# Letting the builder order a two-block network by its timeline simulation

## The chip, the cores and the metric

One core of a Trainium2 chip runs the whole network. The metric is the device time of one execution in microseconds, as the median of the runs shown; less is better.

## The reference

The input is 512 tokens of 1024 channels in float32. The first block has two layers; each mixes the tokens in four groups of 256 channels (RWKV7 "A", differential attention "B", spatial gating "C", forgetting attention "D") and goes through a gated feed-forward part with a short convolution. The second block has one layer: gated linear attention over the tokens and a context of 256, and a mixture of 16 experts, two to a token. Both blocks are modulated by six vectors each, made from a condition by a 1024 by 6144 product.

```python
# first block, for each of two layers
mod = cond @ ada_w[l] + ada_b[l]
h = _rms_norm(x, norm1_g[l]) * (1.0 + sc1) + sh1
pa, pb, pc, pd = _split(h @ w_in[l], GROUP_COLS)
y = jnp.concatenate([ya, yb, yc, yd], axis=-1)     # the four mixers
x = x + g1 * (y @ w_out[l])
h = _rms_norm(x, norm2_g[l]) * (1.0 + sc2) + sh2
x = x + g2 * _conv_glu_ffn(h, ffn_up[l], ffn_conv[l], ffn_conv_b[l], ffn_down[l])
# second block
y_lat = _gla_mixer(h, hc, w_in, w_ga, w_gb, b_g, norm_g, w_out, ctx_out)
x = x + g1 * y
for e in range(N_EXPERTS):
    he = jax.nn.silu(h @ w1[e]) * (h @ w3[e])
    out = out + gates[:, e:e + 1] * (he @ w2[e])
return _rmsnorm(x + g2 * out, final_g)
```

## The kernel before

The kernel is written as a program of tiles: it names the engine of each instruction and the tiles that it reads and writes. The builder then makes one queue of instructions for each engine. To find the order in a queue, the builder plays the program through in a simulation of its own: whenever an engine can take an instruction there, it takes, of those whose inputs are there and whose output has a free buffer, the one that stands first in the program. What the simulated clock says of the length of each instruction thus decides which of two independent instructions comes first. The order is fixed when the program is built, and each engine is handed its queue in that order. Buffers are given out in the order that the simulation finds as well.

The kernel leaves the order to the builder in some places and ties it in others.

- `weave` writes the steps of several generators into the program in turn, so many of one to so many of another (`W_A`, `W_B`, `W_P`, `W_D`, `START`). It makes the program order, and so the rank, of the parts of a mixing stage; it does not fix the queue.
- `first_write` links the first writers of all tiles of one tag: no buffer of a tag is taken ahead of its turn. Tags are linked each for itself; between two tags there is no link.
- In the stage of the experts, the loads of weights are linked one behind the other on SyncE's queue (`load`, `self.loaded`), a few instructions are linked behind a named one (`behind`, `self.normed`, `self.placed`), and the arithmetic of the routing and of the final norm stands in `tc.manual_schedule(engines={Act, DVE})`, where ScalarE and VectorE keep the order as written.

```python
# first_write, with tag the (pool, tag) of the tile that is written for the first time
if tag in self.chain:
    self.tc.add_manual_dep(ins, self.chain[tag], NOSYNC, reason="slots in program order")
self.chain[tag] = ins.name
# mix: the steps of mixer A beside the attention steps, the other projections and the modulations
weave((a_steps, W_A[l]), (then(b_mix, d_mix), W_D[l]), (then(d_project, lambda: a_pair(1), c_mix, close), W_P[l]),
      *([(self.filling(FILL[l]), FILL[l])] if FILL[l] else []), others=True)
weave((a_steps, W_B[l]), (most_out(), 8))
# kernel
with tile.TileContext(nc) as tc:
    network(tc, A, out[0])
```

The stages follow each other: modulation and norm (0 to 130 us), the mixers of layer 0 (130 to 529), its feed-forward part (541 to 927), the mixers of layer 1 (985 to 1366), its feed-forward part (1390 to 1779), gated linear attention (1806 to 2165), the routing (to 2238), the experts (to 2545) and the end.

All products with weights are made from two parts: a weight piece of 512 KB is loaded to `wraw` (or `e_w`), ScalarE casts it to `whi`, VectorE subtracts to get `wlo`, and TensorE makes three products for each pair of operands, into PSUM tiles of the tag `mm`. There are three buffers each of `wraw`, `whi`, `wlo` and `mm`.

In a mixing stage, mixer A is one long chain of small steps for each of two pairs of heads (`mixer_a`): products into tiles of the tag `sa`, each followed by VectorE or ScalarE on tiles `ka`, `a_W`, `a_st`, `X`, then the next small product; in the middle a detour over memory to GpSimd and back (`an_d`, `a_nb`, `t_d`). The scores of the attention mixers B and D go to tiles of the tag `sm`. The projections (`mm`) are the work that can be put between. Every instruction is issued through one wrapper, so the profile puts almost all of them on line 122; they are told apart by the names of their tiles.

Of the kernel before, what the change touches and what calls it, by code (L numbers as in the profile page):

```python
# [29 lines left out]
P = 128  # L30
# [18 lines left out]
# the share of each part of a layer's mixers in turn  # L49
# [60 lines left out]
class Engine:  # L110
    """an engine whose instructions take the tiles of a tag in program order"""
# [31 lines left out]
def weave(*parts, rounds=None, others=False):  # L143
    """steps of several parts in turn; parts: (generator, its number of steps), which yield True while they wait for another;
    rounds: stop when the last part has made that many; others: stop when the first part alone is left"""
    parts = [[g, n, 0] for g, n in parts]
    first, last = parts[0], parts[-1]
    while parts and not (others and parts == [first]):
        for x in sorted(parts, key=lambda q: q[2] / q[1]):
            x[2] += 1  # L150
            try:
                if next(x[0]):
                    x[2] -= 1
                    continue
            except StopIteration:
                parts.remove(x)
            break
        if rounds and last[2] > rounds:
            return


class Modulation:
    """columns r0..r1 of silu(c) @ w + b, 512 channels at a time; parts: (silu(c), last row, column tile) each"""
# [10 lines left out]
    def at_once(self, r0, r1):  # L174
        """eight columns of a single part: r0.. by TensorE, r1.. by VectorE"""
# [31 lines left out]
    def step(self, shared=False):  # L207
        """the sums over partitions of the last four columns, and the products of the next four (shared: by ScalarE and GpSimd, for a single part)"""
# [34 lines left out]
class Net:  # L243
# [46 lines left out]
    def unordered(self, x):  # L290
        """for a tile whose users wait for nothing that comes after it"""
        self.pending.pop(x.tensor.name if hasattr(x, "tensor") else x.name)

    def first_write(self, out, r):
        """the first writers of the tiles of a tag issue in program order, so that no slot is taken ahead of its turn"""
# [10 lines left out]
    def behind(self, **after):  # L306
        """what an engine does in here comes after the named instruction"""
# [20 lines left out]
    def scratch(self, tag, n=S):  # L328
        """2 KB in each partition"""
# [11 lines left out]
    def m4(self):  # L341
        """4 KB in each partition, for mixers B, C and D"""
        return self.t(self.mp, [P, 4 * GW], F32, "m4", self.bufs["m4"])

    def rsqrt(self, x, w, tag="rs"):
        """1/sqrt of a small [128, w] tile, by Newton steps from a bit-level seed"""
# [41 lines left out]
    def a_lora(self, mp, lo):  # L388
        """tanh of the decay inputs (rows 0-31), the a inputs (rows 32-63) and sigmoid of the gate inputs (rows 64-127)"""
# [8 lines left out]
    def mixer_a(self, pool, jj, r, k, v, th, prm, lora, lng, lnb, done):  # L398
        """in steps; done(y) takes the result [128 tokens, tile, 128 channels]"""
# [44 lines left out]
        # k' = k (1 + (a - 1) k_a), a = tanh / 2 + 1/2  # L444
# [169 lines left out]
    def diagonal(x):  # L614
        """the [16, 16] blocks on the diagonals of eight [128, 128] matrices in DRAM, 129 rows apart"""
# [3 lines left out]
    def a_blocks(self, pool):  # L619
        """(I - N)^-1 of the diagonal blocks of the eight strictly lower triangular N, and its transpose, by substitution on GpSimd"""  # L620
# [20 lines left out]
    def a_inverse(self, q, anT):  # L641
        """the transpose of (I - N)^-1 for four of the N (anT: transposed), by merging blocks"""
# [30 lines left out]
    def group_rms(self, x, groups, width, tag):  # L673
        """1/rms of each group of columns, [128, groups]"""
# [9 lines left out]
    def rope_tables(self, pool, qg, kg):  # L684
        """[128, tile, (q, k), 32] tables of cos * g and of the signed sin * g of the partner"""
# [16 lines left out]
    def b_qk(self, i, m, x, tabs, qkT):  # L702
        """x: q (i = 0) or k (1) of the token tiles 2m and 2m + 1 [128, 2 x 256]; their roped transposes go to qkT [128, 4, 512]"""
# [17 lines left out]
    def to_rows(self, x, out, scale=1.0):  # L721
        """two token tiles of 256 channels [128, 2 x 256] to [128, 2, 256] by channel"""
# [6 lines left out]
    def softmax(self, ps, N, mx, lsum, p):  # L729
        """p = exp(ps - max), with its row sums"""  # L730
# [4 lines left out]
    def weigh(self, po, z, p, nb, v):  # L735
        """values v by the weights p [128 queries, 128 nb keys], by channel, to half z of po [2 x 64, 128]"""
# [24 lines left out]
    def b_attend(self, i, qkT, v, nlam, oT):  # L761
        """one block of 128 queries; v: [128, tile, 256]; oT: [128, pair of heads, 512]"""
# [29 lines left out]
    def b_norm(self, oT, g):  # L792
        """rms norm of each head, in place; oT: [128 (two heads), pair, 512]"""
# [31 lines left out]
    def mixer_c(self, m, x, wT, lng, lnb, sgb, out):  # L825
        """x: v of the token tiles 2m and 2m + 1 [128, 2 x 256]; the mixed values by channel to out [128, 2, 512]"""
# [36 lines left out]
    def d_forget(self, ps, fb):  # L863
        """ps: forget logits [head, 512]; the summed log gates, negated, in three bf16 parts [3, head, 512] at partitions 0 and 64"""
# [43 lines left out]
    def w_split(self, ap):  # L908
        """ap: [rows, n] in DRAM; for each 128 rows the two parts [128, n]"""
# [17 lines left out]
    def mm3(self, ps, w, x, start, stop):  # L927
        """ps += w^T x for operands split in two parts"""
# [14 lines left out]
    def cond(self, aps):  # L943
        """silu of vectors of 1024 as columns [128, 8]"""
# [13 lines left out]
    def squares(self, x, kc):  # L958
        """adds up the squares of the channel tiles; with the last, their means by token [128, 8] (PSUM), in two parts"""
# [19 lines left out]
    def rms_tokens(self, pc, tag="nm"):  # L979
        """1/rms of each token [128, 4] from the means of squares"""  # L980
# [6 lines left out]
    def rms_rows(self, pc):  # L987
        """the same in every partition [128, 512] (PSUM)"""
# [7 lines left out]
    def norm_mod(self, x, pq, g, sc, sh, hi, lo):  # L996
        """hi + lo = rms_norm(x) g (1 + sc) + sh; pq: the sums of squares"""
# [22 lines left out]
    def project_rows(self, w, h, m, ntok=S, skip=None):  # L1020
        """one tile of 128 output channels: [128, ntok] = (w columns m)^T h, without the input tile skip"""
# [8 lines left out]
    def project_tokens(self, w, h, n, ps, c0, cols):  # L1030
        """one tile of 128 tokens by `cols` output channels"""
# [43 lines left out]
    def bcast(self, pool, tag, ap, n):  # L1075
        """a vector of n in every partition"""
# [4 lines left out]
    def mix(self, l, h, prm, mp, X, new_y, mods):  # L1081
# [14 lines left out]
        # columns: r 0-255, k 256-511, v 512-767, (wd, ad, gd) 768-895  # L1096
# [5 lines left out]
        def by_token(c0, use):  # L1102
            """256 columns for the pairs of token tiles"""
# [16 lines left out]
        def a_done(j):  # L1120
            """y[j]: [128 tokens, tile, 128 channels] to channel tile j of yT"""
# [29 lines left out]
        sgb = self.t(mp, [P, 2, P], F32, "sgb")         # the bias of the two heads of a pair, in their partitions  # L1151
# [81 lines left out]
        def most_out():  # L1233
            """x + g1 (y w_out) without the channels of the second pair of heads of A"""
# [65 lines left out]
    def fill(self, n, shared=False):  # L1300
        """goes on with the modulations that later parts need"""
# [50 lines left out]
    def load_x(self, src, X, ntok):  # L1352
        """tokens by channel [ntok, 1024] to X [128, 8, ntok]"""
# [11 lines left out]
    def gla_low(self, h, wga, ntok, tag):  # L1365
        """low-rank gate inputs, direction z in rows 32z..32z+15"""
# [8 lines left out]
    def gla_gate(self, low, wgb, bg, hd, z, ntok, out, chunk):  # L1375
        """prefix sums in chunks of 16 times the log decay min(x, 0) - ln(1 + exp(-|x|)); out [128, chunks, chunk + 1], with a leading 0"""
# [18 lines left out]
    def gla_context(self, T, mods, g, put):  # L1395
        """the context normed and modulated, by channel, in steps; put takes its two parts"""
# [36 lines left out]
    def gla_state(self, k, v, pre, S0):  # L1433
        """the states of one head after the context in both directions, in steps; k by channel, v by token"""
# [21 lines left out]
    def gla(self, X, pq, mods, mods_c, cols, new_x):  # L1456
        """X + g1 * mixer(X); X by channel"""
# [3 lines left out]
        with tc.tile_pool(name="gla", bufs=1, reuse_waits="tile") as gp:  # L1461
            T = lambda shape, tag, bufs=1, dt=F32: self.t(gp, shape, dt, "g_" + tag, bufs)
            self.mp, self.bufs = gp, dict(kb=8)
            # memory in the order in which the weights of the experts can have it
# [20 lines left out]
            # one table set with exp and ln, in place of a switch for each  # L1485
# [12 lines left out]
            def silu(ps, out):  # L1498
                """x / (1 + exp(-x)) with the functions of that set; below -80 it is 0"""
# [10 lines left out]
            def feed(hd):  # L1510
                """what head hd needs, in steps"""
# [52 lines left out]
            def result(hd):  # L1564
                """the output of a head by channel, in two parts"""
# [9 lines left out]
            def most_out():  # L1575
                """x + g1 (y w_out) without the channels of the last head"""
# [25 lines left out]
            # what the mixture of experts adds to: a row for each token, and more for the empty slots  # L1602
# [18 lines left out]
    def gla_head(self, gp, hd, q, k, pre, S0, vt, rt):  # L1621
        """one head: its normed and gated output replaces its columns of rt"""
# [7 lines left out]
        # between tiles: decayed keys by token, decayed queries by channel  # L1630
# [27 lines left out]
        # scores [key, tile, query]: every pair of tokens of a tile at the level where their halves part  # L1658
# [34 lines left out]
        # the diagonal, once from each direction  # L1693
# [44 lines left out]
    NE = 16  # L1738
    XB = 7      # the most blocks of 128 tokens that the experts can need beyond one each
# [717 lines left out]
```

## Time and profile before

| | |
|---|---|
| runs | 2612.86 and 2592.25 us, median 2602.56 |
| span of the profiled execution, first to last instruction | 2605.9 us |
| TensorE busy | 2331.5 us (89%) |
| TensorE's weight loads busy | 1865.2 us (72%) |
| VectorE, ScalarE, GpSimd busy | 1724.7, 1072.7, 415.7 us |
| mean granted TensorE clock | 0.913 |

A time of its own for the profiled execution is not given; its span lies between the two runs, 3.3 us above their median. Busy shares are of the span. "PE" is TensorE's matmuls, "PEld" its weight loads, "DVE" VectorE, "ACT" ScalarE, "POOL" GpSimd, "SP" SyncE, whose queue issues nearly all loads; a granted clock of 1.00 is 2.4 GHz and 0.50 is 1.2 GHz.

### The profile page before, as it was taken

The page shows a single profiled execution, that of the slowest core. Times are in us where ns is not written, and L with a number is a line of the kernel's source. Part 1 is how long each engine was busy: PE and PEld are TensorE (multiplying, and loading weights), DVE is VectorE, ACT ScalarE, POOL GpSimd, SP SyncE. Part 2 cuts the span into 40 slices and gives each one's busy share as a digit, 9 for nine tenths or more (in the row PEclk, how much of TensorE's full clock was granted, in tenths as well). Part 3 has the DMA queues.
Part 4 walks back from the last instruction along what each step waited for, and adds up shares of the span by engine and source line. Part 5 has one row for each costly group of instructions (what it writes and reads, how often), then busy time and mean ns, then how long its engine had stood idle before and what let it go on. Part 6 is the DMA issues. An engine that isn't in the chain of part 4 may idle for free.

```text
span 2605.9 us, 33466 instructions
## 1 busy us (share of the span) xinstructions
PE 2331.5 (89%) x12050; PEld 1865.2 (72%) x12050; DVE 1724.7 (66%) x3404; ACT 1072.7 (41%) x1704; POOL 415.7 (16%) x388
## 2 busy tenths in 40 slices
PE   6979889989999988989998999998988885888896
PEld 3767566778888776756676778886887763666685
DVE  5545575577647575455456873765667787898987
ACT  2424445244334342332424432434544433656664
POOL 1212232000000001000100000000222123555712
PEclk7878789989999987887898999998999998999998
DMA  7522234236545542110222563643311035899994
GB/s 243 151 72 74 74 102 133 81 97 183 154 121 182 163 126 60 26 31 27 72 73 67 157 191 110 184 140 110 98 34 48 25 130 202 290 309 321 320 321 104
DMA packets 336872, 352.23 MB, mean 135 GB/s; under 512 B 34006, under 2 KB 245658, under 8 KB 336570
## 3 DMA queue, kind: packets, MB, share of 16 engines
q1 hardware_dynamic: 330922, 330.59, 39.8%
q0 software_dynamic: 5776, 19.42, 3.3%
q8 instruction: 97, 1.59, 0.3%
q14 instruction: 77, 0.63, 0.1%
HBM read 324.74 MB, written 25.17 MB: 134 GB/s over the span
## 4 chain that ended last, share of the span: by engine, by line
PE 53%; DVE 15%; DMA 5%; issue 3%; ACT 2%; POOL 1%; SPq 0%; DVEq 0%; ACTq 0%; POOLq 0%
PE mm L122 40%; PE sa L122 6%; PE sm L122 6%; DVE kb L122 4%; DVE wlo L122 3%; DMA gw<-in_w_mod_dram 3%; DVE gacc L122 1%; DVE hhi L122 1%; DVE r_oh L122 1%; ACT kb L122 1%; DMA gw<-in_ada_w_dram 1%; ACT whi L122 1%; DVE ka L122 0%; POOL a_nb L122 0%; DVE hlo L122 0%
## 5 line engine op out<-in xcount | busy, mean ns | idle before, releaser
L122 ACT CAST whi<-wraw 128x1024 fp32r<-128x1024 f32 (+3 forms) x268 | 260.4, 972 | 524.5 <-PE mm L122 515.3
L122 DVE TENSOR_TENSOR wlo<-wraw,whi 128x1024 fp32r<-128x1024 f32 (+3 forms) x264 | 307.7, 1167 | 244.9 <-ACT whi L122 241.2
L122 PE MATMUL mm<-hhi,whi 128*128 128x512 f32 (+1 forms) x1120 | 452.7, 406 | 13.8 <-ACT hhi L122 6.9
L122 PE MATMUL mm<-hlo,whi 128*128 128x512 f32 (+1 forms) x1120 | 449.1, 402 | 1.7 <-DVE hlo L122 1.6
L122 PE MATMUL mm<-hhi,wlo 128*128 128x512 f32 (+1 forms) x1120 | 447.5, 401 | 3.1 <-DVE wlo L122 3.1
L122 PE MATMUL mm<-whi,hhi 128*128 128x256 f32 (+1 forms) x1100 | 349.2, 341 | 0.5 <-DVE e_a L122 0.5
L122 PE MATMUL mm<-wlo,hhi 128*128 128x256 f32 (+1 forms) x902 | 292.9, 325 | 14.9 <-DVE wlo L122 13.0
L122 PEld LDWEIGHTS mm<-hhi,whi 128*128 128x128 f32 (+1 forms) x1120 | 213.9, 192 | 68.3 <-ACT hhi L122 8.2
L122 PEld LDWEIGHTS mm<-hhi,wlo 128*128 128x128 f32 (+1 forms) x1120 | 213.7, 191 | 53.4 <-DVE wlo L122 4.7
L122 PEld LDWEIGHTS mm<-hlo,whi 128*128 128x128 f32 (+1 forms) x1120 | 214.5, 191 | 49.3 <-DVE hlo L122 3.6
L122 PEld LDWEIGHTS mm<-whi,hhi 128*128 128x128 f32 x1100 | 223.2, 204 | 20.3 <-issue 3.1
L122 PE MATMUL mm<-whi,hlo 128*128 128x256 f32 x704 | 210.4, 299 | 0.0
L122 PEld LDWEIGHTS mm<-wlo,hhi 128*128 128x128 f32 x902 | 184.2, 204 | 31.7 <-DVE wlo L122 18.2
L122 DVE SCALAR_TENSOR_TENSOR gacc<-gw,ct,gacc 128x512 f32<-128x512 f32 x196 | 144.3, 746 | 63.4 <-DMA gw<-in_w_mod_dram 33.7
L122 POOL TENSOR_TENSOR kb<-kb,kb 128x512 f32<-128x512 f32 x12 | 17.4, 1452 | 1015.6 <-ACT kb L122 1015.6
L122 ACT ACTIVATE kb<-kb 128x512 f32<-128x512 f32 (+2 forms) x174 | 103.7, 605 | 181.2 <-DVE kb L122 175.4
L122 PEld LDWEIGHTS mm<-whi,hlo 128*128 128x128 f32 x704 | 144.0, 205 | 1.6 <-issue 1.4
L122 PE MATMUL mm<-f_hi,whi 128*128 128x512 f32 x352 | 140.7, 400 | 1.1 <-DVE kb L122 1.1
L122 PE MATMUL mm<-f_lo,whi 128*128 128x512 f32 x352 | 139.6, 397 | 0.2 <-DVE f_lo L122 0.2
L122 PE MATMUL mm<-f_hi,wlo 128*128 128x512 f32 x352 | 139.2, 396 | 0.0
L122 DVE SCALAR_TENSOR_TENSOR kb<-mm,prm,kb 128x511 f32<-128x511 f32 (+1 forms) x178 | 132.1, 744 | 1.0
L122 ACT CAST whi<-e_w 128x1024 fp32r<-128x1024 f32 x95 | 99.4, 1051 | 63.5 <-PE mm L122 29.9
(594 smaller groups left out, 4284.6 us busy)
## 6 DMA issues: line engine op xcount, KB each, us to landing
wraw<-in_ffn_up_dram SPq DMA_DIRECT2D x88, 512.0 KB
gw<-in_ada_w_dram SPq DMA_DIRECT2D x160, 256.0 KB
gw<-in_w_mod_dram SPq DMA_DIRECT2D x96, 256.0 KB
e_w<-in_w_up_e_dram SPq DMA_DIRECT2D x47, 512.0 KB
wraw<-in_w_in_dram SPq DMA_DIRECT2D x46, 512.0 KB
e_w<-in_w_gate_e_dram SPq DMA_DIRECT2D x43, 512.0 KB
e_w<-in_w_down_e_dram SPq DMA_DIRECT2D x37, 512.0 KB
wraw<-in_ffn_down_dram SPq DMA_DIRECT2D x32, 512.0 KB
```

The lines of the kernel that those rows point to most:

```text
L122: r = f(*args, **kw)
```

## The change

One argument is given to the tile context. With it the builder still plays the program through and takes the ready instruction that stands first in the program, but the simulation that tells it what is ready, and when, is another one: its timeline simulation, with its own lengths for instructions and transfers. The program of tiles, its instructions, links and numbers of buffers are the same; what can differ is the order in each queue, and with it which buffer an instruction gets. The rest of the diff takes comments and docstrings out.

```diff
-    with tile.TileContext(nc) as tc:
+    with tile.TileContext(nc, schedule_with_timeline_sim=True) as tc:
         network(tc, A, out[0])
```

## Rows read from the trace of the kernel before

**Rows 1.** The page: busy time of each engine, and the chain by engine.

```profile
PE 2331.5 (89%) x12050; PEld 1865.2 (72%) x12050; DVE 1724.7 (66%) x3404; ACT 1072.7 (41%) x1704; POOL 415.7 (16%) x388
...
PE 53%; DVE 15%; DMA 5%; issue 3%; ACT 2%; POOL 1%; SPq 0%; DVEq 0%; ACTq 0%; POOLq 0%
```

**Rows 2.** Busy time by stretch (us): length, engines, granted clock, DMA share, GB/s.

```profile
130.00:529.00 399.00, 348.90 (x2043) 266.51 (x2043) 231.26 (x626) 159.29 (x324) 80.31 (x112) 0.86 0.30 88
...
541.00:927.00 386.00, 379.14 (x1699) 311.80 (x1698) 248.48 (x358) 143.77 (x192) 3.80 (x4) 0.99 0.52 154
...
985.00:1366.00 381.00, 349.15 (x2011) 267.18 (x2010) 197.32 (x599) 122.48 (x265) 20.22 (x64) 0.83 0.17 47
...
1390.00:1779.00 389.00, 383.40 (x1714) 314.83 (x1714) 256.58 (x355) 144.88 (x192) 4.17 (x9) 0.99 0.48 145
...
1806.00:2165.00 359.00, 317.33 (x1967) 275.89 (x1967) 246.49 (x490) 149.34 (x277) 73.83 (x59) 0.96 0.22 70
...
2238.00:2545.00 307.00, 275.73 (x1267) 218.28 (x1267) 278.33 (x358) 200.40 (x224) 156.34 (x69) 0.97 0.93 315
```

**Rows 3.** The chain of waits by line, from 985 to 1366 us.

```profile
by line: PE mm L122 37.4%; PE sa L122 20.1%; PE sm L122 18.0%; POOL a_nb L122 2.8%; POOL a_nt L122 2.3%; issue 2.0%; DVE ka L122 1.6%; DMA a_nb<-an_d 1.5%; DMA ka<-t_d 1.4%; ACT kp L122 1.3%; DMA t_d<-a_nb 1.3%; ACT whi L122 1.3%; DMA an_d<
```

**Rows 4.** Pieces of that chain: start, length (us), engine, tile, count.

```profile
985.84 7.29 PE mm L122 x40
...
996.44 0.90 PE sa L122 x6
...
1044.96 6.19 PE mm L122 x52
...
1075.72 2.82 PE mm L122 x24
...
1180.05 5.53 PE mm L122 x24
...
1326.33 0.66 PE mm L122 x2
1326.99 1.38 PE sa L122 x16
...
1340.02 1.64 PE sa L122 x16
1341.66 23.68 PE mm L122 x104
```

**Rows 5.** Timeline of TensorE at two places: start, length (us), instruction.

```profile
1045.47 0.28 PE L122 MATMUL mm<-whi,hlo 128*128 128x256 f32 x1
1045.59 0.28 PE L122 MATMUL mm<-whi,hhi 128*128 128x256 f32 x1
...
1229.20 0.41 PE L122 MATMUL mm<-wlo,hhi 128*128 128x256 f32 x1
1229.41 0.41 PE L122 MATMUL mm<-whi,hlo 128*128 128x256 f32 x1
```

**Rows 6.** Busy time by stretch, as in rows 2, late in layer 1's mixers.

```profile
1172.70:1303.00 130.30, 120.59 (x581) 87.77 (x581) 67.68 (x213) 46.24 (x89) 11.26 (x32) 0.76 0.17 50
```

**Rows 7.** Waits of SyncE's queue, whole span: total us, times, longest.

```profile
SPq L122 <- DVE wlo L122: 934.7, 274, 42.8
SPq L122 <- POOL gacc L122: 140.1, 53, 11.2
...
SPq L122 <- PE sm L122: 63.2, 13, 15.3
```

**Rows 8.** The chain of waits by line, from 1806 to 2165 us.

```profile
by line: PE mm L122 37.1%; DVE kb L122 21.4%; PE sm L122 12.4%; issue 5.5%; PE sa L122 3.0%; ACT kb L122 2.7%; DVE g_rsy L122 2.2%; DVE g_AT L122 2.1%; DVE g_pre L122 2.0%; DVE g_rsu L122 1.8%; DVE wlo L122 1.5%; DVE g_r L122 1.3%; POOL kb 
```

## The prediction

> **What bounds the kernel now.** I read the busy table first, then the stretches, then the chain of waits inside the stretches that order can touch. TensorE's matmuls fill 89% of the span and carry 53% of the chain that ended last, VectorE 15% [rows 1]. So the question for any order is what TensorE does next. The stretches say where that question is open [rows 2]. In the two feed-forward parts TensorE is busy 379.14 of 386 us and 383.40 of 389, at a granted clock of 0.99: there is next to no idle time, and only one kind of work in its queue. In the stage of the experts the DMA share is 0.93 at 315 GB/s: what bounds it is loads, which are linked one behind the other in the program. Three stretches are left where several independent kinds of work compete: the mixers of layer 0 (348.90 of 399 us busy, clock 0.86), those of layer 1 (349.15 of 381, clock 0.83) and the linear attention (317.33 of 359, clock 0.96).
>
> In layer 1's mixers the chain is three quarters TensorE, but not of one kind: 37.4% projections (`mm`), 20.1% the small products of mixer A (`sa`), 18.0% the scores (`sm`) [rows 3]. The reader is to see here that a step of mixer A which is ready has to stand behind the projections that the builder put ahead of it. I went through the pieces of this chain: 67 of them are `sa`, the first and the last at 996.44 and 1340.02 us, and 76 are `mm` before the last long one, the first at 985.84 [rows 4]. Most of the 76 are short, as the two matmuls of 0.66 us between steps of mixer A at 1326.33. Nine are runs of 23 matmuls or more, such as 24 in 2.82 us, 24 in 5.53 us and 52 in 6.19 us [rows 4]. So today the order is fine-grained where the chain is tightest, and in nine places a whole group of projections goes first.
>
> **The change part by part.** The argument adds and removes no instruction, wait or transfer that the program names; all it moves is places in the queues, of every engine and of SyncE's loads. The trace of before shows nothing of the new order, so each stretch gets a bound from both sides.
>
> *Mixers, both layers.* A different simulated clock finds other moments at which a step of mixer A is ready. Where it thinks the step is ready later than before, a group of projections that was behind it goes ahead; TensorE then works through that group before it comes to the step, and what waits for the step is VectorE's and ScalarE's next piece of mixer A, with the rest of that chain behind it. One such group costs 2.82 us with the clock full and 5.53 us with it low [rows 4]; I take the mean, 4.18 us. The spacing of the same matmul shows the two ends: the starts are 0.12 us apart at 1045 us and 0.21 us apart at 1229 us [rows 5]. The projections done early do not shorten the stage, because mixer A is what runs on to its end: the last `sa` piece stands at 1340.02 us, and only the 104 matmuls of 23.68 us that need its result come after [rows 4]. How many groups move cannot be read from the trace. The nearest row to a number is the count of such runs in the present order, nine of 76; I take nine more, as many again: 9 x 4.18 = 38 us. Layer 0's mixers lie before the part that the chain view reaches, but have the same work (2043 matmuls against 2011) in a like stretch [rows 2], so again 38 us, 76 us in both. Upper end: every second of the 67 visits is put behind a group, 33 x 4.18 = 138 us a layer, 276 us in both. Lower end: half of the idle time goes, (50.1 + 31.9)/2 = 41 us from busy times against lengths [rows 2], and a part of the low clock with it, 26 us (worked out under the faster rival): -67 us.
>
> A sentence of the Trainium skill bears on this price. From 1172.7 to 1303 us the granted clock is 0.76 while matmuls are recorded for 120.59 of 130.30 us [rows 6]. The Trainium skill ("TensorE: Matmul & The Clock Gate", HAM oscillation) says that idle gaps between groups of matmuls drop the array to its lower clock, and that the next group then starts slowly. By that rule bunched projections would leave a sparser queue behind them, each moved group would be paid at the low clock, 18 x 5.53 = 100 us in place of 76, and the sum would be 2707 us in place of 2683. The row agrees in part only: the clock is low there, yet the records show few idle gaps.
>
> *Linear attention.* The chain is 37.1% projections and 21.4% VectorE on the level steps (`kb`), with 3.0% `sa` [rows 8]. It alternates between engines, so one moved group costs the same 4.18 us, but there are few places for it. I take one, 4 us. Ends: half the idle time of 41.7 us [rows 2], -21 us, and one group in each of four heads, +17 us.
>
> *Feed-forward parts.* Nothing: one kind of work, cover complete. Ends: the idle time of 6.9 + 5.6 us [rows 2] goes or doubles, -12 and +12 us.
>
> *Experts.* Nothing: loads are linked, and ScalarE's and VectorE's order of the routing is written by hand. But VectorE is busy 278.33 of 307 us there [rows 2], so a few of its small instructions ahead of a `wlo` split would hold TensorE. Ends: TensorE's idle time of 31.3 us is halved or doubled, -15 and +31 us.
>
> *SyncE's queue.* It waits 934.7 us for `wlo` to free a weight buffer, 140.1 us for GpSimd's sums of the modulations and 63.2 us for `sm` [rows 7], in one queue. Between two tags no link holds the order, so a modulation's or mixer's transfer may move ahead of a weight piece and hold the pieces behind it. The most that this can hide behind is the feed-forward parts' twelve microseconds above and the seams; I cost it at nothing within those ends, and take one group, 4 us either way, for the 385 us of the span outside the six stretches.
>
> *Sum.* 2605.9 us of span + 76 + 4 = 2686 us. The median of the runs is 3.3 us under that span: **2683 us**. All ends together would be 2484 and 2943 us, too far for every part to go one way at once.
>
> **The rivals.** *Nothing that counts moves.* For: 775 us of the span are feed-forward at 98% busy, 307 us are bound by loads, the first writers of each tag are linked, and data leaves no choice within a head of the linear attention. Against: two tags share no link, and the fine interleaving of [rows 4] exists only because the simulated clock put it there. That the argument gives in effect the same order belongs here. Time: 2603 us.
>
> *Faster: the new clock is nearer to the chip's.* Place: the queue of TensorE in the mixers and the linear attention. If the timeline simulation knows better when a step of mixer A is ready, runs of 23 and more become fewer than nine and TensorE stands less at a step that is not yet ready. Price: half of the idle time of the three stretches, (50.1 + 31.9 + 41.7)/2 = 62 us [rows 2]. Clocks of 0.86 and 0.83, made of the two levels, mean 112 and 130 us at 1.2 GHz; if a quarter of these 242 us goes to full speed, 0.12 for 0.21 us [rows 5], that is 60 x 0.43 = 26 us. Time: 2605.9 - 88 - 3.3 = 2515 us. It decides from the point at which the runs of 23 or more on the chain fall below nine. Against: the idle time is already spread over short pieces. The weight loads are busy 72% of the span where the matmuls are at 89% [rows 1]. The Trainium skill ("Trainium Kernel Development and Optimization", Reading a trace) calls matmul busy time a bad measure and names the weight loads' share as a good one. By that measure the idle time of the three stretches is 329 us and not 124, and half of it would give some 2438 us. No row shows that idle time as a wait, so I give it no more chance.
>
> *Much slower: the order becomes coarse.* If the new simulation gives TensorE's place away well before the array is free, a ready step of mixer A finds a whole group ahead of it at every second visit. Price: the 276 us above, 2605.9 + 276 + 4 - 3.3 = 2883 us. For: the projections of a tile are all ready together, so there is always a group to take. Against: nothing in the present trace looks like it.
>
> **How the numbers follow.** No change within 2% (2551 to 2655 us, about what a measurement of this kernel can tell) gets 0.27, faster 0.21, the forecast (slower by 2 to 6%) 0.40, much slower 0.12. That is slower 0.52. The range leaves out half of the faster and most of the much slower case: 2540 to 2800 us. The forecast's own range is 2655 to 2760 us.
>
> **What would show it.** Right: the feed-forward stretches keep 386 and 389 us within 12, the experts 307 within 30; the two mixing stretches grow by 25 to 55 us each, more runs of 23 or more `mm` stand on their chain, their clock is no higher. Wrong: mixing stretches that shrink with a clock over 0.86; growth in the feed-forward or expert stretches, which would mean that SyncE's order of loads or VectorE's order matters more than TensorE's.

## The result, and the profile after

The changed kernel takes 2685.24 us (2678.84 and 2691.65), against 2602.56 before: 1.032 times as long, interval 1.026 to 1.037, from two runs of each. The profiled execution is the run of 2691.65 us, with a span of 2689.6 us, 83.7 us more than before's 2605.9. In what follows, runs of over 1.5% above the fastest of their kernel are left out of the ratios and not of the medians; the profiled run of the first experiment, e1_pe_mix, is one of them (2686 us, the others 2646 to 2679), so its stages may be 7 to 40 us high in all.

First the page of the changed kernel: busy time of each engine, and the chain by engine (as [rows 1]).

```profile
PE 2380.0 (88%) x12050; PEld 1909.2 (71%) x12050; DVE 1723.2 (64%) x3404; ACT 1069.8 (40%) x1704; POOL 412.0 (15%) x388
...
PE 62%; DVE 19%; DMA 9%; ACT 4%; issue 4%; POOL 2%; SPq 0%; DVEq 0%; ACTq 0%; POOLq 0%
```

The counts of instructions are those of before. TensorE is busy 48.5 us longer with the same 12050 matmuls, and the clock shown below is lower in five stretches of six. The two lines on the chain are not to be compared: before's reaches back to 529 us only (its shares add up to 79%), this one to the start. Then the six stretches, placed at the same instructions as in [rows 2] (length, then busy time of TensorE, its weight loads, VectorE, ScalarE and GpSimd, granted clock, DMA share, GB/s):

```profile
132.00:574.00 442.00, 382.74 (x2054) 292.50 (x2052) 226.89 (x625) 160.39 (x323) 77.25 (x108) 0.76 0.27 78
592.00:983.00 391.00, 381.95 (x1701) 314.31 (x1701) 244.76 (x352) 142.35 (x190) 3.87 (x4) 0.98 0.51 150
1043.00:1446.00 403.00, 358.58 (x2009) 276.11 (x2007) 197.81 (x596) 122.32 (x265) 17.33 (x64) 0.80 0.16 45
1473.00:1869.00 396.00, 385.87 (x1747) 318.35 (x1746) 255.95 (x357) 144.11 (x191) 4.23 (x9) 0.99 0.48 144
1892.00:2230.00 338.00, 310.09 (x1967) 277.23 (x1966) 242.72 (x490) 147.28 (x276) 79.14 (x59) 0.95 0.23 76
2303.00:2628.00 325.00, 285.09 (x1269) 223.50 (x1270) 285.28 (x360) 198.83 (x225) 152.59 (x69) 0.95 0.89 301
```

The reader is to subtract line by line. Mixers of layer 0: +43 us. Feed-forward part: +5. Mixers of layer 1: +22. Feed-forward part: +7. Linear attention: -21. Experts: +18. The remaining 9.7 us of the 83.7 lie between the stretches. So the two mixing stages do carry the growth, but one stretch became faster, and the forecast gave it +4. In layer 0's mixers 34 of the 43 us are busy time of TensorE (382.74 against 348.90, for 11 matmuls more), at a clock of 0.76 in place of 0.86; in layer 1's it is 9 of the 22 us.

Now who ends the mixing stage of layer 1. The chain of waits by line, and four of its pieces (start, length in us, engine, tile, count):

```profile
by line: PE mm L122 36.1%; PE sm L122 21.8%; PE sa L122 19.4%; DVE kp L122 1.7%; issue 1.7%; DVE ka L122 1.6%; DVE wlo L122 1.4%; ACT kp L122 1.1%; POOL a_nb L122 1.1%; DVE b_mx L122 1.0%; POOL a_nt L122 1.0%; ACT whi L122 1.0%; DVE d_mx L1
...
1214.58 10.02 PE mm L122 x43
...
1377.34 3.17 PE sa L122 x16
...
1415.26 1.98 PE sm L122 x8
...
1418.24 27.40 PE mm L122 x113
```

In [rows 4] the last `sa` piece, at 1340.02, stands directly ahead of the closing 104 matmuls. Here the last `sa` piece stands at 1377.34, which counted from the start of the stage is 21 us earlier than before (334 us against 355). What stands ahead of the closing matmuls is `sm`, the scores of attention, at 1415.26, 38 us after mixer A's last piece. The time of `sm` on the chain rose from 69 to 88 us, that of `sa` stayed (77 and 78).

And what TensorE has to do beside these last steps. Stretches at the end of the stage, first with all instructions, then with those on `mm` tiles alone (columns as above):

```profile
1331.00:1360.00 29.00, 27.38 (x154) 17.64 (x152) 9.30 (x35) 6.32 (x23) 0.00 (x0) 0.65 0.00 1
1360.00:1389.00 29.00, 24.96 (x107) 15.19 (x106) 13.69 (x53) 5.64 (x18) 0.00 (x0) 0.50 0.00 0
1389.00:1417.00 28.00, 20.23 (x65) 12.16 (x65) 8.00 (x21) 4.30 (x10) 0.00 (x0) 0.62 0.00 1
...
1331.00:1360.00 29.00, 0.00 (x0) 0.00 (x0) 0.00 (x0) 0.00 (x0) 0.65 0.00 1
1360.00:1389.00 29.00, 0.00 (x0) 0.00 (x0) 0.00 (x0) 0.00 (x0) 0.50 0.00 0
1389.00:1417.00 28.00, 4.21 (x9) 2.81 (x9) 0.00 (x0) 0.00 (x0) 0.62 0.00 1
```

The kernel before, at its end of the same stage, in the same two forms:

```profile
1282.00:1311.00 29.00, 28.63 (x178) 21.11 (x177) 16.36 (x29) 15.02 (x28) 0.00 (x0) 1.00 0.29 91
1311.00:1339.00 28.00, 28.00 (x207) 19.45 (x205) 11.72 (x38) 7.90 (x20) 0.00 (x0) 1.00 0.18 57
...
1253.00:1282.00 29.00, 12.17 (x49) 8.87 (x50) 0.76 (x2) 0.60 (x1) 0.65 0.16 41
1282.00:1311.00 29.00, 9.02 (x37) 6.01 (x36) 0.68 (x1) 1.18 (x2) 1.00 0.29 91
1311.00:1339.00 28.00, 15.37 (x47) 7.49 (x45) 1.50 (x2) 0.00 (x0) 1.00 0.18 57
```

For 58 us the changed kernel has no projection left: only steps of mixer A and of attention, at a granted clock of 0.65 and then 0.50, which is 1.2 GHz. Before, 9 and 15 us of projections stand beside the same kind of steps from 1282 us on, and the clock is 1.00. That is no rule: in the 29 us ahead of these, before has 12.17 us of projections and a clock of 0.65. Layer 0 of the changed kernel ends the same way: no `mm` from 448 to 511 us, at 0.68 and 0.50.

The queue itself shows where the projections went. This is the share of a stretch's projections (by the time of the `mm` matmuls in each kernel's own trace) that stand ahead of a given part of attention's `sm` matmuls on TensorE:

| ahead of | layer 0 before | layer 0 after | layer 1 before | layer 1 after |
|---|---|---|---|---|
| half of attention's matmuls | 0.50 | 0.64 | 0.52 | 0.68 |
| three quarters | 0.66 | 0.81 | 0.70 | 0.83 |

The projections moved ahead of attention. (The expectations below count all work of layer 1's stage: 69% before, 82% after.) In the whole span, VectorE's waits for a score and ScalarE's for its row maximum grew, before and then after:

```profile
DVE d_mx L122 <- PE sm L122: 48.3, 25, 5.2
ACT kp L122 <- DVE d_mx L122: 39.6, 18, 6.7
```

```profile
ACT kp L122 <- DVE d_mx L122: 90.8, 23, 10.7
DVE d_mx L122 <- PE sm L122: 78.9, 30, 5.5
```

### The profile page after: what moved, and what is told of

Same layout as the page of the kernel before. It is cut to its first block, busy times and chain, and to the rows that moved or that the text cites. A ratio compares the mean times of both kernels' runs of the same rounds, so it can differ in the third digit from the quotient of the medians.

```text
span 2689.6 us, 33526 instructions
## 1 busy us (share of the span) xinstructions
PE 2380.0 (88%) x12050; PEld 1909.2 (71%) x12050; DVE 1723.2 (64%) x3404; ACT 1069.8 (40%) x1704; POOL 412.0 (15%) x388
## 4 chain that ended last, share of the span: by engine, by line
PE 62%; DVE 19%; DMA 9%; ACT 4%; issue 4%; POOL 2%; SPq 0%; DVEq 0%; ACTq 0%; POOLq 0%
PE mm L122 43%; PE sm L122 9%; PE sa L122 9%; DVE kb L122 4%; DVE wlo L122 4%; DMA gw<-in_ada_w_dram 3%; DMA gw<-in_w_mod_dram 2%; DVE gacc L122 2%; ACT whi L122 1%; DVE hhi L122 1%; DVE ka L122 1%; DMA whi<-in_ada_w_dram 1%; DVE r_oh L122 1%; ACT kb L122 1%; POOL gacc L122 1%
## 5 line engine op out<-in xcount | busy, mean ns | idle before, releaser
L122 DVE TENSOR_TENSOR wlo<-wraw,whi 128x1024 fp32r<-128x1024 f32 (+3 forms) x264 | 300.8, 1141 | 244.5 <-ACT whi L122 240.9
```

Of the source, the lines that this page charges most:

```text
L122: r = f(*args, **kw)
```

## The experiments

Both kernels build the same instructions under the same names, so the order of one can be forced on the other. All twelve kernels do this, with order-only links along a list of names; only the list, the queues and the stages differ. Nothing is left out of the computation.

```diff
+def as_listed(net, tc):
...
+    for name in QUEUES:
...
+        for s in STAGES:
+            a, b = net.marks[s], net.marks[s + 1]
+            mine = [n for n in listed if a <= n < b]
...
+            for x, y in zip(mine, mine[1:]):
+                tc.add_manual_dep(found[y], found[x].name, NOSYNC, reason="as listed")
```

Stages 1 and 3 are the mixers, 5 is the linear attention, 6 the routing and the experts. The other queues are planned anew around the linked one.

To compare them I cut each profiled execution where VectorE last writes the residual `X` of a stage, which holds the seams as well. Times in us; the ratio is to runs of the kernel before on the same chip.

| kernel | to end of mixers 0 | feed-forward | mixers 1 | feed-forward | linear attention | rest | median | ratio (interval) |
|---|---|---|---|---|---|---|---|---|
| before | 525 | 393 | 457 | 405 | 400 | 427 | 2603 | |
| after | 569 | 404 | 483 | 410 | 378 | 445 | 2685 | 1.032 (1.026 to 1.037) |
| e1_pe_mix | 573 | 408 | 468 | 414 | 376 | 445 | 2669 | 1.022 (1.014 to 1.031) |
| e2_mm_sm | 565 | 405 | 447 | 412 | 377 | 443 | 2650 | 1.018 (1.012 to 1.024) |
| e3_mm_sa | 595 | 405 | 485 | 414 | 378 | 442 | 2719 | 1.043 (1.037 to 1.049) |
| e4_sp | 567 | 397 | 478 | 409 | 376 | 443 | 2671 | 1.026 (1.020 to 1.032) |
| e5_act_mix | 578 | 406 | 526 | 410 | 376 | 444 | 2740 | 1.053 (1.050 to 1.056) |
| e6_pe_act_mix | 547 | 402 | 454 | 411 | 378 | 444 | 2634 | 1.011 (1.007 to 1.015) |
| e7_all_mix | 523 | 405 | 442 | 410 | 379 | 443 | 2619 | 1.009 (1.006 to 1.012) |
| e8_gla | 524 | 392 | 454 | 401 | 381 | 425 | 2576 | 0.990 (0.987 to 0.993) |
| e9_pe_dve_mix | 549 | 409 | 444 | 410 | 376 | 443 | 2634 | 1.015 (1.010 to 1.020) |
| e10_mix_moe | 535 | 407 | 454 | 412 | 377 | 429 | 2616 | 1.005 (1.001 to 1.009) |
| e11_gla_pe | 526 | 393 | 451 | 403 | 387 | 428 | 2591 | 0.995 (0.992 to 0.998) |
| e12_gla_vec | 525 | 392 | 452 | 401 | 394 | 431 | 2597 | 0.998 (0.995 to 1.000) |

How far to trust a cell: the third column of the four kernels that leave the mixers as in before (before, e8, e11, e12) reads 451 to 457, and e7, which has the same order there, 442 in the fastest of its executions (2604 us). Each cell comes from one execution.

**TensorE's order in the mixers.**

```diff
+STAGES = (1, 3)
+QUEUES = ('PE',)
```

> The changed kernel, with TensorE's queue in the two mixing stages linked in the order that it has in the kernel before; the other queues are left to the timeline simulation. Three theories. TensorE's order in the mixers is the cause: the stages give back their growth of 43 and 22 us, the time is 2685 - 65 = 2620 us (2610 to 2632). The order on VectorE and ScalarE is the cause: less than a third comes back, over 2663 us. The order of loads on SyncE is the cause: nothing comes back, 2685 us.

The median is 2669 us, 17 us under the changed kernel; by the ratio of 1.022 it is 25 us. The first theory falls. The second, less than a third back and over 2663 us, fits the median and misses the ratio by little. The intervals of e1_pe_mix and of the changed kernel overlap (1.014 to 1.031, 1.026 to 1.037), so this run alone does not settle that TensorE's order is a cause at all.

**Which pair on TensorE.** The same, with a list that holds only the instructions that write `mm` and `sm`, and then only those that write `mm` and `sa`.

> The changed kernel; of TensorE's queue in the two mixing stages only the projections (mm) and the steps of the attention mixers (sm) are linked in the order of the kernel before; mixer A (sa) is free to stand where the timeline simulation puts it. Theory 'attention is late' (three quarters of the attention's steps stand behind 82% of the stage's work in place of 69%, so that the stage ends on attention with no projections left beside it): at least 45 of the 65 us come back, 2640 us or less. Theory of the prediction (steps of mixer A stand behind groups of projections): mixer A is not helped, at most 15 us come back, 2670 us or more.

> The changed kernel; of TensorE's queue in the two mixing stages only the projections (mm) and the steps of mixer A (sa) are linked in the order of the kernel before; attention (sm) is free. Theory of the prediction (steps of mixer A stand behind groups of projections): at least 45 of the 65 us come back, 2640 us or less. Theory 'attention is late': three quarters of its steps still stand behind 79% of the stage's work (69% before, 82% after), so about a quarter comes back, 2665 to 2675 us.

With projections and attention in the old order the time fell to 2650 us, between the two forecasts, and layer 1's column from 483 to 447, all of its growth. With projections and mixer A in the old order it rose to 2719 us, which neither theory had. So "attention is late" is shown for layer 1, and not for layer 0, whose column stayed at 565. The prediction's theory falls for layer 1 by the trace of the changed kernel, where mixer A was early. e3_mm_sa is no test of it, because mixer A was not helped there. This is where TensorE ends the last product of mixer A and the last score of attention (us; layer 0 from the start of the program, layer 1 from the end of the feed-forward part ahead):

| kernel | layer 0, mixer A | layer 0, attention | layer 1, mixer A | layer 1, attention |
|---|---|---|---|---|
| before | 491 | 463 | 424 | 396 |
| after | 500 | 531 | 407 | 444 |
| e2_mm_sm | 543 | 506 | 418 | 399 |
| e3_mm_sa | 560 | 520 | 451 | 420 |
| e5_act_mix | 549 | 511 | 497 | 460 |
| e6_pe_act_mix | 514 | 484 | 421 | 393 |
| e9_pe_dve_mix | 516 | 487 | 411 | 383 |
| e7_all_mix | 488 | 460 | 407 | 380 |

Of these only the changed kernel ends its mixers on attention. In layer 0 of e2_mm_sm attention ends 25 us earlier than in the changed kernel, though still 43 us later than before, and mixer A ends 43 us later than in the changed kernel. Six groups of projections stand between its last steps, as the prediction had it for the changed kernel. The chain there, some of its longest pieces:

```profile
498.25 3.65 PE sa L122 x26
508.77 4.64 PE mm L122 x19
514.79 3.95 PE mm L122 x17
519.79 4.76 PE mm L122 x20
524.93 5.67 PE mm L122 x24
530.86 4.99 PE mm L122 x21
536.10 5.21 PE mm L122 x22
```

The six take 29 us.

The end of layer 1's mixers in e2_mm_sm, all instructions and then `mm` alone, has its projections and its clock again:

```profile
1324.00:1353.00 29.00, 27.05 (x169) 18.83 (x167) 14.67 (x34) 16.27 (x29) 0.00 (x0) 1.00 0.21 73
1353.00:1381.00 28.00, 27.24 (x173) 19.82 (x173) 11.87 (x31) 8.38 (x19) 0.00 (x0) 1.00 0.19 53
...
1324.00:1353.00 29.00, 12.90 (x51) 8.87 (x51) 0.67 (x1) 1.79 (x3) 1.00 0.21 73
1353.00:1381.00 28.00, 13.98 (x56) 10.31 (x57) 1.50 (x2) 0.00 (x0) 1.00 0.19 53
```

**SyncE's order of loads, whole program.**

```diff
+STAGES = (0, 1, 2, 3, 4, 5, 6)
+QUEUES = ('SP',)
```

> The changed kernel with SyncE's queue linked in the order of the kernel before, stage by stage, over the whole program; the queues of the compute engines are left to the timeline simulation. Theory 'order of loads': the growth outside the mixers (18 us in the experts, 12 in the feed-forward parts) and part of that in the mixers comes back, 2655 us or less. Theory 'TensorE's order': the mixers keep their growth; at most the 18 us of the experts come back, 2667 to 2690 us.

2671 us, in the range of the second theory, but not where it put it: the experts kept 443 us, and the feed-forward part of layer 0 gave back 7 us (404 to 397). Layer 0's mixers kept their growth.

**Layer 0: a second queue.** There ScalarE and GpSimd also make modulations from loads of `gw`, and ScalarE waited for these 43.5 us in the mixers of the changed kernel against 18.9 before. Hence ScalarE alone, and ScalarE with TensorE.

```diff
+STAGES = (1, 3)
+QUEUES = ('ACT',)
```

> The changed kernel, with ScalarE's queue alone linked in the order of the kernel before in the two mixing stages; TensorE's and VectorE's are left to the timeline simulation, which then follows ScalarE's order (three quarters of the attention's steps stand behind 69% of the stage's work again). Theory 'ScalarE waits for modulation loads' (layer 0's mixers keep their growth with TensorE's order put back, and ScalarE's waits for the loads of gw there are 35 to 44 us against 19 before): the end of layer 0's mixers falls from 569 us to 545 or less, layer 1's stretch to 465 or less, the time to 2645 or less. Theory 'it takes TensorE's exact order': both stretches stay within 10 us of the changed kernel's, 2675 us or more.

```diff
+STAGES = (1, 3)
+QUEUES = ('PE', 'ACT')
```

> The changed kernel, with TensorE's and ScalarE's queues linked in the order of the kernel before in the two mixing stages. Theory 'ScalarE waits for modulation loads': what TensorE's order alone did not give back in layer 0 comes back, the end of layer 0's mixers falls from 569 to 540 us or less, 2635 us or less. Theory 'VectorE's order': layer 0's mixers still end at 560 us or later, 2655 us or more.

ScalarE alone is the slowest kernel of all, 2740 us, although attention's place in TensorE's queue was about that of before (0.66 of layer 1's projections ahead of three quarters of its matmuls, 0.70 before). Both theories fall with it. Its mixers end on mixer A, in layer 1 90 us later than in the changed kernel (497 against 407), so attention's place alone does not make a stage short. ScalarE and TensorE together ended layer 0's mixers at 547 us, between the two forecasts, and took 2634 us. That fits ScalarE's waits as well as it fits any queue that agrees with TensorE's, so the counterpart has to tell.

```diff
+STAGES = (1, 3)
+QUEUES = ('PE', 'DVE')
```

> The changed kernel, with TensorE's and VectorE's queues linked in the order of the kernel before in the two mixing stages, ScalarE's left free: the counterpart of the run with TensorE and ScalarE, where layer 0's mixers ended at 547 us against 573 with TensorE alone. Theory 'ScalarE's order around the modulation loads is the second cause in layer 0': they still end at 560 us or later here, with ScalarE's waits for gw at 35 us or more. Theory 'any second queue that agrees with TensorE helps': 550 us or earlier.

Layer 0's mixers end at 549 us, as with ScalarE, just inside the second theory, although ScalarE's waits for `gw` stay longer. These waits from 130 to 580 us, of e6_pe_act_mix and then e9_pe_dve_mix (us, times, longest):

```profile
ACT gw L122 <- DMA gw<-in_ada_w_dram: 22.5, 12, 5.7
```

```profile
ACT gw L122 <- DMA gw<-in_ada_w_dram: 32.5, 21, 3.1
```

With 10 us more of these waits the stage ends 2 us later, and in e5_act_mix, where they were 21.0 us, it ended at 578. So the waits for modulation loads are not the second cause. A second queue that agrees with TensorE's is worth the same with either of the two tried.

```diff
+STAGES = (1, 3)
+QUEUES = ('PE', 'DVE', 'ACT', 'POOL', 'SP')
```

> The changed kernel, with all five queues linked in the order of the kernel before in the two mixing stages. If the growth of these stages is a matter of order alone, their 65 us come back (layer 0's mixers end at 527 to 535 us, 2610 to 2630 us in all); if it comes from what stands around them (the prologue's order, loads ahead of the stage), layer 0's mixers still end at 550 us or later.

2619 us, and both mixing columns are at before's level or under it: their growth is a matter of order, and not of what stands around them. (Order here takes in which buffer a tile gets; the runs do not part the two.)

**The experts.**

```diff
+STAGES = (1, 3, 6)
+QUEUES = ('PE', 'DVE', 'ACT', 'POOL')
```

> The changed kernel, with the queues of TensorE, VectorE, ScalarE and GpSimd (not SyncE's) linked in the order of the kernel before in the two mixing stages and in the routing and the experts. Theory 'the experts grow by the order of the compute engines': their stretch falls from 445 to 432 us or less, 2600 to 2612 us in all. Theory 'they grow by SyncE's order of loads': 440 us or more there, 2615 us or more in all.

The last column fell from 445 to 429 us with SyncE's queue left free, so the experts grew by the order of the compute engines. The total, 2616 us, is 4 us over this theory's forecast and at the edge of the other's; the stretch decides between them.

**The gain in the linear attention.** Here the order of the changed kernel is forced on the kernel before, with all queues, with TensorE's alone, and with VectorE's and ScalarE's alone.

```diff
+STAGES = (5,)
+QUEUES = ('PE', 'DVE', 'ACT', 'POOL', 'SP')
```

> The kernel before, with all five queues of the linear attention linked in the order that the changed kernel has there. If the 22 us that the changed kernel gains in this stretch are a matter of its order, 2604 - 22 = 2582 us (2572 to 2592), faster than both kernels. If they come from something ahead of the stage, or from a run's clock, no change, 2597 to 2612 us.

> The kernel before, with TensorE's queue alone linked in the order of the changed kernel in the linear attention. Its stretch takes 400 us before and 381 with all queues of the changed kernel. Theory 'TensorE's order brings the gain': 388 us or less. Theory 'VectorE and ScalarE make the level products earlier (TensorE's waits of sm for VectorE's kb are 14 us in place of 27)': 395 us or more.

> The kernel before, with VectorE's and ScalarE's queues alone linked in the order of the changed kernel in the linear attention. Theory 'TensorE's order brings the gain': 395 us or more in its stretch (400 before, 381 with all queues of the changed kernel). Theory 'VectorE and ScalarE make the level products earlier': 388 us or less.

All queues: 2576 us, 1.0% faster than before, the fastest kernel here. By the stage column TensorE's order alone brings 13 of the 19 us, the other two 6 (394 us, between the two forecasts), which is no more than equal kernels differ by in one column; by the ratios (0.990, 0.995, 0.998) TensorE's order brings about half. TensorE's waits of `sm` for VectorE's level products `kb`, from 1790 to 2170 us, in before, e8_gla, e11_gla_pe and e12_gla_vec in turn:

```profile
PE sm L122 <- DVE kb L122: 26.8, 23, 2.4
```

```profile
PE sm L122 <- DVE kb L122: 14.0, 10, 6.7
```

```profile
PE sm L122 <- DVE kb L122: 13.5, 5, 5.8
```

```profile
PE sm L122 <- DVE kb L122: 22.7, 14, 8.0
```

With the new order TensorE stands 13 us less at a score whose `kb` VectorE has not made. But ScalarE and GpSimd make `kb` too, and with these TensorE's waits for `kb` are 30.6, 17.0, 26.0 and 25.8 us: 14 us less with all queues, and 5 with either part. So the gain is shown to be a matter of the order in this stage, and TensorE's order to be a good part of it; that the waits for `kb` explain TensorE's part is not shown.

## Why the prediction was right, and where it was not

The time was right, 2683 us against 2685. Much of that is sum, and not insight, so step by step:

- *Mixers, +76 us.* Measured +43 and +22, 65 us. The place was right, and the signs that it named: clocks of 0.76 and 0.80 against 0.86 and 0.83 and, on layer 1's chain, 13 runs of 23 or more projections ahead of the closing one, against nine. Layer 0 grew within 25 to 55 us, layer 1 just under that. The mechanism failed at the step "what waits for the step is VectorE's and ScalarE's next piece of mixer A". Mixer A of layer 1 finished 21 us earlier in its stage, that of layer 0 only 7 us later (368 against 361 us into it, of 43 us of growth). The steps that came to stand behind projections were those of attention; the projections were then used up, and the stage ran out on two thin chains at the low clock. e2_mm_sm shows this for layer 1. The count of nine more groups has no support: four more such runs stand on the chain.
- *"Mixer A is what runs on to its end"* was read from [rows 4]. It held for before and for the six kernels with linked queues in the table above, and not for the changed kernel. In before the last `sm` piece stands only 27 us ahead of the last `sa` (1313.09 and 1340.02). Of two chains that end so close, either can be the one that ends the stage once the order is new.
- *The low clock.* The rule of the Trainium skill ("TensorE: Matmul & The Clock Gate", HAM oscillation), that idle gaps between groups of matmuls drop the array to its lower clock, gave 2707 us, with the misread 5.53 us as its price. The trace agrees with it in part again: the clock is at 0.50 from 1360 to 1389 us, where matmuls are recorded for 24.96 of 29 us, so there is little idle time.
- *Linear attention, +4 us.* Measured -21, the very end of its range. What happened is the faster rival, in one of its three places: half of the idle time of 41.7 us, 21 us, was its price there. That the price fits is partly luck: the idle time fell by 14 us (to 27.9), the other 7 are busy time of TensorE (310.09 against 317.33).
- *Feed-forward parts, 0 within 12.* +5 and +7, within. e4_sp gives 7 us of layer 0's back with SyncE's order, so the linked first writers did not fix everything.
- *Experts, 0 from -15 to +31.* +18. The sentence that a few instructions out of place would hold TensorE points the right way, as TensorE's idle time rose from 31.3 to 39.9 us, half of the growth; that it was the compute engines and not the loads is shown by e10_mix_moe and e4_sp. Which instructions they are stays open.
- *The rest, 0 within 4.* +9.7, missed, most of it (6 us) at the norm behind layer 0's mixers.

The price of a group, which enters the 76 and the 2707 us, was misread. The 24 matmuls of 5.53 us at 1180.05 did not run at the low clock: the granted clock there is 1.00, and they have 512 columns where the 24 of 2.82 us have 256. The stretch of the first (columns as in [rows 2]), and one matmul of each:

```profile
1180.05:1185.58 5.53, 5.53 (x27) 4.51 (x26) 4.97 (x16) 1.77 (x4) 0.00 (x0) 1.00 0.00 0
...
1180.18 0.39 PE L122 MATMUL mm<-hhi,whi 128*128 128x512 f32 x1
...
1076.11 0.28 PE L122 MATMUL mm<-wlo,hhi 128*128 128x256 f32 x1
```

So 4.18 us is a mean of two shapes, not of two clocks. By the spacing of 0.21 us [rows 5], 24 matmuls of 256 columns would take 5.0 us at the low clock, an estimate that comes close to the 5.53 by luck. The pieces of the chain were also counted a little high: from 985 to 1366 us there are 63 of `sa` and 71 of `mm` ahead of the last, not 67 and 76, so the upper end would be 31 visits, 260 us in both layers. The nine runs are right.

So the sum came out by errors that cancel: 76 + 4 forecast, 65 - 21 + 5 + 7 + 18 + 10 measured. The rival "nothing that counts moves" fell, and so did the coarse order at 2883 us.

What stays open is layer 0. With TensorE's projections and attention in the old order it kept its growth (565 us): its end passed from attention to mixer A, with groups of projections ahead of the last steps. With TensorE and one more queue half of the growth went (547 and 549), with all five all of it (523). Two of the lists for one queue made the kernel worse than the changed one (e3_mm_sa, e5_act_mix), and both times mixer A came late. What held mixer A back there, and in e6 and e9, the runs do not isolate.

## What to carry to other kernels

A builder's simulated clock is a setting of the schedule to be measured stage by stage: here one stage gained 6% and two lost 6 to 11%, and the best kernel took each stage from the clock that did it better. Where several chains end close together, ask of each of them what happens if it becomes the last, and what is left to run beside it; filler that is used up early is missed at the end. An order belongs to all queues at once: taken over for one queue alone it can be worse than either original.

## What the runs showed that I had not expected

- The same 2009 matmuls of layer 1's mixers, within two, were busy 358.58 us in the changed kernel and 349.15 before: the order of work moved the clock that the stage was granted, 0.80 against 0.83. Over its whole column the clock was 0.81 in the changed kernel and 0.82 in e4_sp, and 0.84 to 0.88 in the five traces with the old order on all queues or close to it (before, e7, e8, e11, e12).
- Putting the projections back beside attention in layer 0 moved the end of the stage to mixer A and gained 4 us of the 44 (565 against 569, before 525).
- Forcing ScalarE's old order alone cost more than the whole change (ratio 1.053 against 1.032), with layer 1's column at 526 us against 457 and 483 in the two originals.
